# Moving the mixers' two-tensor operations from Pool to DVE in a two-layer network of token mixers

## The chip, the cores and the metric

The kernel runs on one core of a Trainium2 chip. The metric is the device time of one execution in microseconds. Five engines with queues of their own work side by side: TensorE (PE in the profile, with its weight loads as PEld), VectorE (DVE), ScalarE (ACT), GpSimd (POOL, here Pool) and SyncE (SP), which issues nearly all DMAs. Each engine runs its instructions in the order of its queue; an instruction that waits for a semaphore holds up what stands behind it.

## What is computed

The reference is a network of two layers on 256 context and 256 latent tokens of width 1024, in float32. Each layer is: a gated FFN (width 2816) with residual and layer norm; a token mixer; a second FFN. In the last layer only the latent tokens go on.

```
u @ w_in -> columns for three mixers, and three gates
a: gated delta rule, 4 heads, chunks of 128, forward and backward:
   conv + silu of q, k, v; solve (I + A) X = [b v, b exp(g) k];  S = c S + k_w^T u;  o = q S + P u
b: retention with rotary q, k and fixed decays, 4 heads, both directions; head norm; silu gate
c: state-space mixer, 16 heads in 2 groups, both directions:
   o = (scores * decay) (x * step) + decayed state + d * x;  silu gate; group norm
merged = g0 * (ya @ w_a) + g1 * (yb @ w_b) + g2 * (yc @ w_c);   out = merged @ w_out
```

The term `d * x` of mixer c is the skip term.

## The kernel before

Tokens lie along the free axis: 512 columns while both streams are needed, 256 in the second layer where only latent tokens are. Weights come as 1313 blocks of 128x512, in the order of use, through `raw_block` (L104). `wtile` (L113) splits a block: ACT casts it to a high half `whi` (L121), and DVE or Pool subtracts to give the low half `wlo` (L123). Every product is three matmuls (`mm3`, L138): high x high, high x low, low x high. There are four buffers each of `raw`, `whi` and `wlo`; the three steps are emitted with raised priority, so that the planner of the language, which orders each engine's queue from the program's order, priorities and free buffers, sets them ahead of their use.

Who makes `wlo` is decided in L122: of each four blocks, Pool takes the first `pool_lo`. This number is 0 in the FFNs. In the mixers it is set stage by stage from the tuple `plo` (L1435): values of 1 to 4 in the six stages of either layer.

`mix_main` (L1431) orders a mixer. The delta rule (`gdn`, L782) runs first, two heads at a time in layer 0 and four in layer 1; its chain of small operations is filled up with projections of the other mixers: `take(us)` (L502) draws so many microseconds of TensorE work from a generator `fill` (the z gates of mixer a, retention, then the projections of mixer c) and emits it at that place of the program. How much is drawn where stands in `gdn_fill` (L1447). The stages of `gdn`: projections with `conv_silu` (L520; four taps on DVE, L534) and transposes; row vectors written to DRAM (`rows_out`, L767) and read back broadcast over the partitions (`rows_in`, L777) as `Rg` and `Rb`; the matrices M and PT per chunk (L899 to L931), with the product of M with `Rb` on Pool (L925) and that of Q on Pool (L936); 32x32 blocks of M sent through DRAM, loaded as B (L951) and inverted in 31 steps of two DVE operations each (L953 to L959); a merge of the blocks to 128x128 (L993); a scan over four chunks (L1054), whose weighted tiles `bv` and `kw` come from Pool (`weighted`, L967), one chunk ahead in layer 0 and with a single buffer in layer 1.

Then `ssd` (L1218), mixer c, runs interleaved with `merge` (L1374), the gates and the three output products. Per group of heads it loads x as one tile `xt` of 1 MB (L1226), makes weighted values V (L1239) and states (L1253, Pool, and L1254), and per chunk and direction a matrix E of 128 x 8 x 128: decay times score mask (L1289), for the forward direction times step (L1291), then plus DI, the identity times `d` (L1292, on Pool). In `merge` a gated product is added to the sum of the mixers before it on Pool (L1423).

Of the kernel before, what the change touches and what calls it, by code (L numbers as in the profile page):

```python
# [8 lines left out]
F32 = mybir.dt.float32  # L9
# [6 lines left out]
P = 128  # L16
# [30 lines left out]
class Net:  # L47
# [84 lines left out]
    ahead = True  # L132
# [466 lines left out]
    def retention(self):  # L599
# [13 lines left out]
        def table(h):  # L613
# [10 lines left out]
            nc.gpsimd.tensor_tensor(out=tab[:, 1], in0=te2, in1=tab[:, 1], op=ADD)  # L624
# [157 lines left out]
    def gdn(self, H, gp, pool0, gtok):  # L782
# [6 lines left out]
        nu, no = 2 * nh, len(och)  # L789
# [93 lines left out]
        self.take(wt[1])  # L883
# [4 lines left out]
        with ExitStack() as st:  # L888
            pp = st.enter_context(tc.tile_pool(name=f"gprep{tag}", bufs=1, side="right", reuse_waits="tile"))
            for p in range(0, nh, 2):  # L890
                Rg = pp.tile([P, 2, 2, T], F32, tag="Rg", name="Rg")
                Rb = pp.tile([P, 2, 2, T], F32, tag="Rb", name="Rb")
                for d in range(2):
                    self.rows_in(Rg[:, d], self.dR[d * 20 + h0 + p:d * 20 + h0 + p + 2, :])
                    self.rows_in(Rb[:, d], dB[d * nh + p:d * nh + p + 2, :])
                nG = pp.tile([P, 4, 2], F32, tag="nG", name="nG", bufs=2)
                nc.vector.tensor_scalar(out=nG, in0=self.G[:, :, 1, h0 + p:h0 + p + 2], scalar1=-1.0, scalar2=None, op0=MUL)
                pair = lambda t, c: t[:, c].rearrange("p (d h) n -> p d h n", d=2)[:, :, p:p + 2]
                for c in range(4):  # L899
# [25 lines left out]
                    nc.gpsimd.tensor_tensor(out=pair(M, c), in0=pair(M, c), in1=Rb[:, :, :, cs], op=MUL)  # L925
# [6 lines left out]
                for d in range(2):  # L932
                    for i in range(2):
                        q_ = Q[:, d, p + i]
                        nc.scalar.activation(out=q_, in_=Rg[:, d, i, self.oc], func=AF.Exp)
                        nc.gpsimd.tensor_tensor(out=q_, in0=q_, in1=qf[:, p + i], op=MUL)  # L936
# [8 lines left out]
        with ExitStack() as st:  # L945
# [6 lines left out]
            nc.sync.dma_start(out=X, in_=self.io["eye32"].rearrange("(o r) c -> o r c", o=1).broadcast_to([n, 32, 32]))  # L952
            for s in range(31):  # L953
# [5 lines left out]
                self.take(wt[3] / 31)  # L959
# [7 lines left out]
        def weighted(s):  # L967
# [4 lines left out]
            for d in range(2):  # L972
                c, us = ch[d], slice(d * nh, d * nh + nh)
                nc.gpsimd.tensor_tensor(out=bv[:, us], in0=vtok[:, c], in1=bcol(d)[:, c].unsqueeze(2).to_broadcast([P, nh, P]), op=MUL)
                if s < 3:
                    nc.gpsimd.tensor_tensor(out=kw[:, us], in0=ktok[:, c], in1=(w0, w1)[d][:, c].unsqueeze(2).to_broadcast([P, nh, P]), op=MUL)
# [241 lines left out]
    def ssd(self):  # L1218
        nc, l, tc = self.nc, self.l, self.tc
        och, oc = self.och, self.oc  # L1220
        with ExitStack() as st:
            pool = st.enter_context(tc.tile_pool(name=f"ssd{l}", bufs=1, side="right", reuse_waits="tile"))
            for g in range(2):
                hs = slice(4 + 8 * g, 12 + 8 * g)
                xt = pool.tile([P, 4, 512], F32, tag="xt", name="xt")
                nc.sync.dma_start(out=xt, in_=self.dx[:, :, g * 512:(g + 1) * 512].rearrange("c p n -> p c n"))  # L1226
# [4 lines left out]
                def weighted(n):  # L1231
                    for d in range(2):
# [6 lines left out]
                        nc.vector.tensor_tensor(out=v, in0=xt[:, c].rearrange("p (h e) -> p h e", h=8),  # L1239
                                                in1=wv.unsqueeze(2).to_broadcast([P, 8, 64]), op=MUL)  # L1240

                def state(n):
                    for d in sorted(V):
# [7 lines left out]
                        else:  # L1251
                            prev = S[d, c].rearrange("p (h e) -> p h e", h=8)
                            nc.gpsimd.tensor_tensor(out=Sn, in0=prev, in1=self.ct[:, c, d, hs].unsqueeze(2).to_broadcast([P, 8, 64]), op=MUL)  # L1253
# [8 lines left out]
                def prep(c, d):  # L1262
# [27 lines left out]
                    if d == 0:  # L1290
                        nc.vector.tensor_tensor(out=e, in0=e, in1=step.unsqueeze(2).to_broadcast([P, 8, P]), op=MUL)  # L1291
# [519 lines left out]
```

## Time and profile before

| | |
|---|---|
| runs | 2748.7, 2752.3, 2749.12 us; median 2749.12 |
| profiled execution | 2749.3 us, span 2747.5 us |
| TensorE busy | 2594.9 us (94% of the span), granted clock 0.98 on the mean |
| DVE busy | 2068.4 us (75%) |
| ACT busy | 1224.9 us (45%) |
| Pool busy | 719.8 us (26%), of which wlo 291.2 |
| HBM read | 401.93 MB, 158 GB/s with what is written |

The span has two mixers, about 450 to 1112 us and 1990 to 2508 us; before, between and after them lie FFNs. Busy time is the union of an engine's instructions. A wait is idle time of an engine, put down to what ended it. Consecutive DVE instructions overlap a little in the records, so the time from one start to the next is shorter than a duration.

### The profile page before, as it was taken

The page shows a single profiled execution, that of the slowest core. Times are in us where ns is not written, and L with a number is a line of the kernel's source. Part 1 is how long each engine was busy: PE and PEld are TensorE (multiplying, and loading weights), DVE is VectorE, ACT ScalarE, POOL GpSimd, SP SyncE. Part 2 cuts the span into 40 slices and gives each one's busy share as a digit, 9 for nine tenths or more (in the row PEclk, how much of TensorE's full clock was granted, in tenths as well). Part 3 has the DMA queues.
Part 4 walks back from the last instruction along what each step waited for, and adds up shares of the span by engine and source line. Part 5 has one row for each costly group of instructions (what it writes and reads, how often), then busy time and mean ns, then how long its engine had stood idle before and what let it go on. Part 6 is the DMA issues. An engine that isn't in the chain of part 4 may idle for free. (4 is left out here: it accounts for less than half of the span.)

```text
span 2747.5 us, 45507 instructions
## 1 busy us (share of the span) xinstructions
PE 2594.9 (94%) x16136; PEld 2214.7 (81%) x16136; DVE 2068.4 (75%) x4078; ACT 1224.9 (45%) x2420; POOL 719.8 (26%) x615
## 2 busy tenths in 40 slices
PE   8999999999999999999999999999988888888998
PEld 6888887777777778898888988888877778778997
DVE  5888868778878684578888778845788876776766
ACT  3333256443455653363332543323655353654553
POOL 2000054432443253340001320002443433463100
PEclk9999999999999999999999999999999999999999
DMA  8666645422525555365665566643635333756665
GB/s 279 184 185 184 183 139 160 132 63 87 171 78 157 165 169 158 111 196 184 194 186 168 158 205 194 185 117 105 180 101 169 106 97 101 197 183 179 202 184 152
DMA packets 292808, 436.06 MB, mean 159 GB/s; under 512 B 42628, under 2 KB 109700, under 8 KB 292452
## 3 DMA queue, kind: packets, MB, share of 16 engines
q1 hardware_dynamic: 292580, 433.16, 53.6%
q8 instruction: 126, 2.06, 0.3%
q14 instruction: 102, 0.84, 0.1%
HBM read 401.93 MB, written 31.13 MB: 158 GB/s over the span
## 5 line engine op out<-in xcount | busy, mean ns | idle before, releaser
L121 ACT CAST whi<-raw 128x512 fp32r<-128x512 f32 x1003 | 614.9, 618 | 825.1 <-PE pd L142 189.4
L123 DVE TENSOR_TENSOR wlo<-raw,whi 128x512 fp32r<-128x512 f32 x803 | 586.8, 733 | 256.9 <-ACT whi L121 249.8
L141 PE MATMUL p<-uh,whi 128*128 128x512 f32 (+1 forms) x1216 | 445.3, 366 | 1.5 <-ACT whi L121 1.5
L143 PE MATMUL p<-uh,wlo 128*128 128x512 f32 (+1 forms) x1216 | 440.2, 362 | 0.2 <-DVE wlo L123 0.2
L142 PE MATMUL p<-ul,whi 128*128 128x512 f32 (+1 forms) x1216 | 440.2, 362 | 0.0
L123 POOL TENSOR_TENSOR wlo<-raw,whi 128x512 fp32r<-128x512 f32 x200 | 291.2, 1460 | 505.0 <-ACT whi L121 463.9
L190 DVE SCALAR_TENSOR_TENSOR acc<-raw,cT,acc 128x512 f32<-128x512 f32 x448 | 320.4, 753 | 81.3 <-DMA raw<-wst 79.3
L141 PEld LDWEIGHTS p<-uh,whi 128*128 128x128 f32 x1216 | 229.1, 188 | 42.9 <-ACT whi L121 5.0
L307 POOL TENSOR_TENSOR y<-y,piv 128x256 f32<-128x256 f32 x30 | 30.9, 1059 | 884.2 <-ACT piv L305 884.2
L143 PEld LDWEIGHTS p<-uh,wlo 128*128 128x128 f32 x1216 | 229.0, 188 | 37.3 <-DVE wlo L123 0.4
L142 PEld LDWEIGHTS p<-ul,whi 128*128 128x128 f32 x1216 | 229.2, 188 | 34.2
L141 PE MATMUL pd<-ach,whi 128*128 128x512 f32 (+1 forms) x660 | 232.0, 352 | 1.5 <-ACT whi L121 1.5
L143 PE MATMUL pd<-ach,wlo 128*128 128x512 f32 (+1 forms) x660 | 229.4, 348 | 0.5 <-DVE wlo L123 0.5
L142 PE MATMUL pd<-acl,whi 128*128 128x512 f32 (+1 forms) x660 | 229.2, 347 | 0.0
L534 DVE SCALAR_TENSOR_TENSOR cacc<-craw,pcol,cacc 128x508 f32<-128x508 f32 (+2 forms) x192 | 170.7, 894 | 15.7 <-ACT cacc L529 14.1
L141 PEld LDWEIGHTS pd<-ach,whi 128*128 128x128 f32 x660 | 125.0, 189 | 19.0 <-ACT whi L121 2.9
L143 PEld LDWEIGHTS pd<-ach,wlo 128*128 128x128 f32 x660 | 125.0, 189 | 16.7 <-DVE wlo L123 0.9
L142 PEld LDWEIGHTS pd<-acl,whi 128*128 128x128 f32 x660 | 125.0, 189 | 15.2
L141 PE MATMUL gate<-uh,whi 128*128 128x512 f32 (+1 forms) x384 | 132.8, 346 | 0.0
L143 PE MATMUL gate<-uh,wlo 128*128 128x512 f32 (+1 forms) x384 | 130.2, 339 | 1.1 <-POOL wlo L123 1.1
L142 PE MATMUL gate<-ul,whi 128*128 128x512 f32 (+1 forms) x384 | 130.3, 339 | 0.0
L411 ACT CAST ach<-pr 128x512 fp32r<-128x512 f32 (+1 forms) x88 | 50.0, 568 | 141.5 <-DVE pr L410 141.5
(476 smaller groups left out, 6015.3 us busy)
## 6 DMA issues: line engine op xcount, KB each, us to landing
raw<-wst SPq DMA_DIRECT2D x1313, 256.0 KB, 2.8
R<-dR SPq DMA_DIRECT2D x24, 512.0 KB, 5.7
dah<-y SPq DMA_DIRECT2D x9, 1024.0 KB, 5.6
y<-dah SPq DMA_DIRECT2D x28, 256.0 KB, 4.8
Rg<-dR SPq DMA_DIRECT2D x8, 512.0 KB, 4.6
Rb<-dB SPq DMA_DIRECT2D x8, 512.0 KB, 4.9
dx<-xo SPq DMA_DIRECT2D x16, 256.0 KB, 3.1
xt<-dx SPq DMA_DIRECT2D x4, 1024.0 KB, 9.0
```

The source lines that it names most:

```text
L121: nc.scalar.copy(out=hi, in_=r)
L123: e.tensor_tensor(out=lo, in0=r, in1=hi.bitcast(F32), op=SUB)
L141: nc.tensor.matmul(out, wh, xh, start=start, stop=False)
L142: nc.tensor.matmul(out, wh, xl, start=False, stop=False)
L143: nc.tensor.matmul(out, wl, xh, start=False, stop=stop)
L190: eng.scalar_tensor_tensor(out=acc, in0=r, scalar=c, in1=acc, op0=MUL, op1=ADD)
L307: (nc.gpsimd if m >= self.ln_dve[0] else nc.vector).tensor_tensor(out=y[:, m, c], in0=y[:, m, c], in1=piv, op=SUB)
L411: nc.scalar.copy(out=F["ach"][:, m], in_=pr[:, :n])
L534: nc.vector.scalar_tensor_tensor(out=a[:, :, lo:hi], in0=r[:, :, lo + d:hi + d], scalar=w[:, tap:tap + 1], in1=a[:, :, lo:hi], op0=MUL, op ...
```

## The change

All two-tensor operations that the mixers had on Pool go to DVE: `plo` becomes zero everywhere, so DVE makes each `wlo`; the products of M (L925) and Q (L936), the tables of retention (L624), the decayed states (L1253) and the additions of `merge` (L1423) change engine. The weighted tiles of the scan stay on Pool, as one-tensor operations with a scalar per partition, one per head. The skip term is added by the operation that multiplies by step. Three pieces are moved or split: the fill of `gdn_fill[1]` comes behind the first issue of `Rg` and `Rb`; a new entry `gdn_fill[8]` of 8 us (layer 0) or 4 us (layer 1) is taken out of the fill of the 31 steps and put ahead of them; and `xt` is four tiles with four loads.

```diff
-            nc.gpsimd.tensor_tensor(out=tab[:, 1], in0=te2, in1=tab[:, 1], op=ADD)
+            nc.vector.tensor_tensor(out=tab[:, 1], in0=te2, in1=tab[:, 1], op=ADD)
...
         self.rows_out(pool0, 40, 40 + nu, dB)
-        self.take(wt[1])
...
                     self.rows_in(Rb[:, d], dB[d * nh + p:d * nh + p + 2, :])
+                if p == 0:
+                    self.take(wt[1])
...
-                    nc.gpsimd.tensor_tensor(out=pair(M, c), in0=pair(M, c), in1=Rb[:, :, :, cs], op=MUL)
+                    nc.vector.tensor_tensor(out=pair(M, c), in0=pair(M, c), in1=Rb[:, :, :, cs], op=MUL)
...
-                        nc.gpsimd.tensor_tensor(out=q_, in0=q_, in1=qf[:, p + i], op=MUL)
+                        nc.vector.tensor_tensor(out=q_, in0=q_, in1=qf[:, p + i], op=MUL)
...
+            ahead = wt[8]
+            self.take(ahead)
             for s in range(31):
...
-                self.take(wt[3] / 31)
+                self.take((wt[3] - ahead) / 31)
...
-                c, us = ch[d], slice(d * nh, d * nh + nh)
-                nc.gpsimd.tensor_tensor(out=bv[:, us], in0=vtok[:, c], in1=bcol(d)[:, c].unsqueeze(2).to_broadcast([P, nh, P]), op=MUL)
-                if s < 3:
-                    nc.gpsimd.tensor_tensor(out=kw[:, us], in0=ktok[:, c], in1=(w0, w1)[d][:, c].unsqueeze(2).to_broadcast([P, nh, P]), op=MUL)
+                c = ch[d]
+                for i in range(nh):
+                    nc.gpsimd.tensor_scalar(out=bv[:, d * nh + i], in0=vtok[:, c, i], scalar1=bcol(d)[:, c, i:i + 1], scalar2=None, op0=MUL)
+                    if s < 3:
+                        nc.gpsimd.tensor_scalar(out=kw[:, d * nh + i], in0=ktok[:, c, i], scalar1=(w0, w1)[d][:, c, i:i + 1], scalar2=None, op0=MUL)
...
-                xt = pool.tile([P, 4, 512], F32, tag="xt", name="xt")
-                nc.sync.dma_start(out=xt, in_=self.dx[:, :, g * 512:(g + 1) * 512].rearrange("c p n -> p c n"))
+                xt = [pool.tile([P, 512], F32, tag="xt", name="xt", bufs=4) for _ in range(4)]
+                for c in range(4):
+                    nc.sync.dma_start(out=xt[c], in_=self.dx[c, :, g * 512:(g + 1) * 512])
...
-                            nc.gpsimd.tensor_tensor(out=Sn, in0=prev, in1=self.ct[:, c, d, hs].unsqueeze(2).to_broadcast([P, 8, 64]), op=MUL)
+                            nc.vector.tensor_tensor(out=Sn, in0=prev, in1=self.ct[:, c, d, hs].unsqueeze(2).to_broadcast([P, 8, 64]), op=MUL)
...
-                        nc.vector.tensor_tensor(out=e, in0=e, in1=step.unsqueeze(2).to_broadcast([P, 8, P]), op=MUL)
-                        nc.gpsimd.tensor_tensor(out=e, in0=e, in1=DI, op=ADD)
+                        for h in range(8):
+                            nc.vector.scalar_tensor_tensor(out=e[:, h], in0=e[:, h], scalar=step[:, h:h + 1], in1=DI[:, h], op0=MUL, op1=ADD)
...
-                    nc.gpsimd.tensor_tensor(out=a, in0=a, in1=pa[:, :no], op=ADD)
+                    nc.vector.tensor_tensor(out=a, in0=a, in1=pa[:, :no], op=ADD)
...
-        plo = self.plo = ((3, 4, 2, 2, 3, 2), (4, 1, 3, 4, 2, 2))[l]
+        plo = self.plo = ((0,) * 6, (0,) * 6)[l]
...
-            self.gdn_fill = ((2, 4, 5, 18, 1, 1, 3, 4), (2, 4, 5, 20, 0.5, 0.35, 3, 4))[self.outs[0]]
+            self.gdn_fill = ((2, 4, 5, 18, 1, 1, 3, 4, 8), (2, 4, 5, 20, 0.5, 0.35, 3, 4, 4))[self.outs[0]]
```

## Rows read from the trace of the kernel before

**Rows 1.** Stretches (two mixers, an FFN): length, each engine's busy us, PE clock, DMA.
```profile
450.00:1112.00 662.00, 625.02 (x3730) 510.14 (x3730) 494.38 (x1036) 319.89 (x646) 254.56 (x200) 0.98 0.44 129
1990.00:2508.00 518.00, 450.67 (x3512) 400.83 (x3511) 396.44 (x802) 270.88 (x575) 227.06 (x171) 0.96 0.49 141
1250.00:1500.00 250.00, 250.00 (x1243) 201.90 (x1243) 214.71 (x380) 75.37 (x134) 0.00 (x0) 1.00 0.64 187
```

**Rows 2.** Waits of PE, 1940 to 2530 us: total us, times, longest.
```profile
PE rof L687 <- DVE on L681: 7.5, 4, 3.1
...
PE br L143 <- POOL wlo L123: 2.6, 3, 1.2
...
PE gate L143 <- POOL wlo L123: 1.1, 3, 0.6
```

**Rows 3.** Twelve slices of 20 us in which DVE is fullest: their sum.
```profile
sum 240.00, PE 209.47 PEld 170.25 DVE 228.83 ACT 118.77 POOL 121.78; mean PE 17.46 PEld 14.19 DVE 19.07 ACT 9.90 POOL 10.15
```

**Rows 4.** DVE by line and shape: second mixer (two rows), FFN stretch (last row).
```profile
L123 DVE TENSOR_TENSOR wlo<-raw,whi 128x512 fp32r<-128x512 f32 x82 | 67.2, 821 | 35.3 <-ACT whi L121 32.5 <-PE gO L1082 1.2 <-PE br L142 1.1
L534 DVE SCALAR_TENSOR_TENSOR cacc<-craw,pcol,cacc 128x508 f32<-128x508 f32 x36 | 36.0, 999 | 6.7 <-ACT cacc L529 6.4
...
L123 DVE TENSOR_TENSOR wlo<-raw,whi 128x512 fp32r<-128x512 f32 x90 | 61.8, 687 | 4.3 <-ACT whi L121 3.9
```

**Rows 5.** Tiles cacc and E, DVE: shortest, median, longest ns; whole span.
```profile
L534 DVE SCALAR_TENSOR_TENSOR cacc<-craw,pcol,cacc x192: 466/745/1816, 450.6 to 2253.3; 128x508 f32<-128x508 f32 x84, 128x510 f32<-128x510 f32 x84, 128x254 f32<-128x254 f32 x12, 128x255 f32<-128x255 f32 x12
...
L907 DVE SCALAR_TENSOR_TENSOR E<-Rg,G,masks x56: 314/417/1434, 491.3 to 2137.0; 128x128 f32<-128x128 f32 x56
...
L1291 DVE TENSOR_TENSOR E<-E,sp x12: 1210/1224/2318, 872.4 to 2442.7; 128x1024 f32<-128x1024 f32 x12
```

**Rows 6.** Timeline, DVE (four rows) and POOL (three): start us, us, instruction.
```profile
507.47 5.52 DVE L907 SCALAR_TENSOR_TENSOR E<-Rg,G,masks 128x128 f32<-128x128 f32 x5
...
2287.33 2.16 DVE L1069 SCALAR_TENSOR_TENSOR bv<-kS,col,bv 128x128 f32<-128x128 f32 x8 [1.22 <-PE kS L1066]
...
2410.45 0.69 DVE L123 TENSOR_TENSOR wlo<-raw,whi 128x512 fp32r<-128x512 f32 x1 [0.18 <-ACT whi L121]
2411.06 0.68 DVE L1342 TENSOR_TENSOR yscl<-O,ysch 128x512 fp32r<-128x512 f32 x1
...
507.36 1.34 POOL L936 TENSOR_TENSOR Q<-Q,qf 128x512 f32<-128x512 f32 x1
508.67 1.33 POOL L925 TENSOR_TENSOR M<-M,Rb 128x512 f32<-128x512 f32 x1
509.96 2.89 POOL L123 TENSOR_TENSOR wlo<-raw,whi 128x512 fp32r<-128x512 f32 x2
```

**Rows 7.** POOL by line and shape, whole span: busy us, mean ns, idle before.
```profile
L123 POOL TENSOR_TENSOR wlo<-raw,whi 128x512 fp32r<-128x512 f32 x200 | 291.2, 1460 | 505.0 <-ACT whi L121 463.9 <-PE sz L143 11.8 <-ACT mW L1006 9.1
...
L1292 POOL TENSOR_TENSOR E<-E,DI 128x1024 f32<-128x1024 f32 x12 | 29.6, 2464 | 34.9 <-DVE E L1291 34.9
L1423 POOL TENSOR_TENSOR gth<-gth,pa 128x512 f32<-128x512 f32 x16 | 24.4, 1528 | 17.8 <-DVE gth L1419 17.8
```

**Rows 8.** The chain that ended last, second mixer (1990 to 2508 us), by line.
```profile
by line: issue 3.5%; DMA R<-dR 2.6%; POOL wlo L123 1.7%; PE sO L1313 1.3%; PE gate L143 1.2%; PE gate L141 1.2%; PE gate L142 1.2%; POOL gth L1423 1.2%; ACT whi L121 0.9%; DMA yt<-dy 0.8%; PE sS L1246 0.7%; ACT E L1280 0.6%; PE br L142 0.5%
```

**Rows 9.** Waits of DVE, whole span: total us, times, longest.
```profile
DVE tm L956 <- DMA B<-d: 9.4, 3, 5.6
...
DVE E L907 <- DMA Rg<-dR: 3.8, 2, 3.3
...
DVE V L1239 <- DMA xt<-dx: 2.8, 2, 2.5
```

**Rows 10.** POOL: two one-input operations (shortest, median, longest ns), timeline of bv.
```profile
L1029 POOL COPY M<-XX x12: 397/457/1109, 585.9 to 2280.3; 128x256 f32<-128x256 f32 x8, 128x512 f32<-128x512 f32 x4
...
L368 POOL TENSOR_SCALAR y<-y,agb x72: 552/994/2032, 395.0 to 2556.5; 128x256 f32<-128x256 f32 x72
...
2284.52 2.49 POOL L974 TENSOR_TENSOR bv<-gvtok,beta 128x512 f32<-128x512 f32 x2 [3.65 <-PE gU L1074]
```

More of the change, by code (lines that the diff above doesn't have):

```diff
@@ L1238, in weighted @@
                         v = V[d] = pool.tile([P, 8, 64], F32, tag="V", name="V", bufs=2)
-                        nc.vector.tensor_tensor(out=v, in0=xt[:, c].rearrange("p (h e) -> p h e", h=8),
+                        nc.vector.tensor_tensor(out=v, in0=xt[c].rearrange("p (h e) -> p h e", h=8),
                                                 in1=wv.unsqueeze(2).to_broadcast([P, 8, 64]), op=MUL)
@@ L1290, in prep @@
                     if d == 0:
-                        nc.vector.tensor_tensor(out=e, in0=e, in1=step.unsqueeze(2).to_broadcast([P, 8, P]), op=MUL)
-                        nc.gpsimd.tensor_tensor(out=e, in0=e, in1=DI, op=ADD)
+                        for h in range(8):
+                            nc.vector.scalar_tensor_tensor(out=e[:, h], in0=e[:, h], scalar=step[:, h:h + 1], in1=DI[:, h], op0=MUL, op1=ADD)
                     else:
                         xb = units[c][4] = pool.tile([P, 8, 64], F32, tag="V", name="xb", bufs=2)
-                        nc.vector.tensor_tensor(out=xb, in0=xt[:, c].rearrange("p (h e) -> p h e", h=8),
+                        nc.vector.tensor_tensor(out=xb, in0=xt[c].rearrange("p (h e) -> p h e", h=8),
                                                 in1=step.unsqueeze(2).to_broadcast([P, 8, 64]), op=MUL)
@@ L1309, in out @@
                                 if kind == "x":
-                                    lh, rh = xb[:, h] if d else xt[:, c, h * 64:(h + 1) * 64], E[d][:, h]
+                                    lh, rh = xb[:, h] if d else xt[c][:, h * 64:(h + 1) * 64], E[d][:, h]
                                 else:
```

## The prediction

> **What bounds the kernel now.** I read the engines' busy times by stretch first. In an FFN stretch (1250 to 1500 us) TensorE is busy all of the time beside a VectorE (DVE) at 86% and an idle GpSimd (Pool). In the two mixer stretches, 1180 us together, TensorE is idle 37.0 + 67.3 = 104 us, and only there is Pool at work, 254.6 and 227.1 us [rows 1]. All that this change can win lies in those 104 us, and in the dips of the clock beside them (0.98 and 0.96 granted against 1.00). Next, whom TensorE waits for there: DVE results, at the end of chains of small operations, in pieces of 1 to 6 us; for a low half of a weight block (wlo) made by Pool only 3.7 us in six waits of the second mixer [rows 2]. So the low halves come in time; late are the mixers' own chains on DVE.
>
> Then slices of 20 us. In twelve of the 59 slices of the mixers DVE has next to no gap: 228.8 of 240 us. In these TensorE loses 30.5 us, 29% of its mixer idle in 20% of the time [rows 3]. Third, why DVE is full: by operation, with the same tile shapes kept apart. A wlo takes 821 ns in the second mixer and 687 in the FFN stretch without Pool; a convolution tap 999 where the median is 745; an E of the decay 314 at its shortest, and up to 1434 [rows 4, 5]. The timeline shows how: from 507.47 five E's need 5.52 us, where eight such operations in a row take 2.16, a step of (2.16 - 0.34) / 7 = 0.26 us; Pool runs two multiplications and two wlo's just then [rows 6]. DVE and Pool take turns. Such lost time (an operation's duration less the shortest tenth of its form, where a Pool instruction lies over it) comes to 177 us over the two mixers, op by op in the timelines; 170 of it under the kinds of Pool operation that this change removes. From the grouped rows alone it is at least 82 x (0.821 - 0.687) + 36 x (0.999 - 0.745) = 20 us for two groups [rows 4, 5].
>
> **Part 1: two-tensor work from Pool to DVE.** Removed from Pool: 200 wlo, 12 skip additions, 32 merge additions, 16 decayed states, 16 M and 16 Q products and 8 tables three of these seven kinds stand in [rows 7]. On DVE an operation costs the step to the next start, not its duration: 2411.06 - 2410.45 = 0.61 us for 512 columns [rows 6]. So 200 wlo cost 122 us, 56 others of 512 columns 34, 24 of 256 columns (0.33 each: half of the columns' share) 8, 8 tables 4. The skip term becomes eight scalar_tensor_tensor of 128 columns, 8 x 0.26 = 2.08, in place of one step product of 1.22 less the overlap of 0.08 that a wlo of 0.69 has with its successor [rows 5, 6]: 12 x 0.94 = 11. Together +179 us on DVE against 170 that it gets back: no net load, and if nothing came back, +179.
>
> What counts is where. The other 47 slices have DVE gaps, which take up what is moved there; in the last 60 to 70 us of either mixer hardly any time is lost now and some 22 us arrive, beside a TensorE that is nearly full. In the twelve full slices I count 60 us lost and 41 arriving (some 450 operations; [rows 6] are the pattern: 4.2 us lost under four Pool operations that will cost 4 x 0.61 = 2.4). That frees 19 us of DVE where TensorE loses 30.5. A freed DVE lets TensorE on only until the next thing is late (the same slices have ACT and transposes in the chain), so I take half: **-10 us**; bounds -19 and, with nothing given back, +41 less the 11 us of gaps, +30.
>
> A page of the Trainium skill, "SBUF — State Buffer", section "Who interferes with whom", says that a DVE instruction with two SBUF inputs contends with any Pool instruction that reads SBUF. It speaks against a part of this change: the one-input operations left on Pool read SBUF too, and there will be 112 of them where 42 stood. The trace has 1 us or less under Pool's copies, which are few; by the page some of the 7 us now lost under those 42 would stay or double, so the term would be -7 in place of -10.
>
> **Part 2: Pool legs in the chains.** A merge addition has to run on Pool between two DVE operations (1.53 us, now 0.61), a skip addition takes 2.46 behind a product of 1.22 (now 2.08 for both) [rows 5, 7]. In the chain that ended last, over the second mixer, Pool's wlo and gth stand with 1.7% and 1.2% of 518 us [rows 8], 15 us; at half of the duration that is **-8 us**. Bounds 0 (the next wait takes over) and -16 (the first mixer, which the chain does not show this way, gains as much).
>
> **Part 3: work set in front of waits.** No TensorE instruction goes; the order does. In the 31-step solve, DVE stands for the block load B: 9.4 us in three waits [rows 9], and the fill's DVE work stands behind it. Eight (second mixer: four) of the 18 (20) us of fill now go in front; their weight loads, casts and wlo's run during the load. The price is that the solve has less fill left for TensorE, 10 us beside some 16 us of DVE steps; but all of it was DVE's time anyway. The Rg/Rb loads go in front of 4 us of fill on SP's queue: four loads of 512 KB are issued before the fill's two or three weight loads, and what waits on SP behind the Rb load (until dB is written) is those weight loads, with four raw buffers ahead. DVE waited 3.8 us for Rg [rows 9]. Sum of these waits 13.2; I take **-6**, bounds -13 and +6 (the fill that the solve then lacks). The four xt loads in place of one: DVE waited 2.8 us for xt [rows 9], **-2**, bounds -3 and +3 (four issues on SP).
>
> **Part 4: what Pool keeps.** The weighted tiles of the scan become 112 per-head operations of 128 columns. The trace has none. Nearest: a copy of 256 columns 397 ns at its shortest, a two-scalar one 552 [rows 10]; so between half of the latter, 0.28, and all of it, 0.55; I take 0.42, near the copy. In the second mixer, with one buffer, this lies on the path: now two bv from 2284.52 to 2287.0, and DVE uses them at 2287.33 [rows 6, 10]. Eight at 0.42 take 3.4, not 2.5: 0.9 later, two such steps, **+2**; bounds 0 and +7 (if each kw stands before the next head's bv). While Pool is late DVE stands in that step, with wlo's queued behind it. In the first mixer there are two buffers, and it hides.
>
> **Sum.** -10 - 8 - 6 - 2 + 2 = -24. The profiled execution took 2749.3 us (span 2747.5), 0.2 from the median of 2749.12: 2725.3, so 2725. Ends of all terms: -51 and +46.
>
> **Rivals.**
> - *A, slower: DVE becomes the engine that decides in the mixers.* If the long durations are not Pool's doing, or the time comes back where nobody waits, DVE goes from 890.8 to 1070 of 1180 us, and the full slices grow by the +30 of part 1: 2779. Low halves then queue behind DVE's own waits, which Pool's never did. For it: full slices exist; the wlo's come first in the order and push the chains. Against it: 687 ns without Pool. It decides once TensorE's waits for DVE in the mixers pass some 90 us. "Perfetto Trace Analysis" of the Trainium skill, "Optimizing Scalar/DVE Operations", says that offloading from a saturated DVE may make sense, and adds that it might not help between these two; the lost time of the rows bears out the addition.
> - *B, slower by a little: the solve runs out of fill and the per-head operations sit in the scan.* +6 and +7 with parts 1 and 2 at nothing and xt at -2: 2760.
> - *C, no change.* DVE's load is even (179 against 170), and what it gains in one slice the moved wlo's take in the next: parts 1 and 2 cancel with each other's bounds, 2748.
> - *D, a larger gain.* The full slices lose their 30.5 us of idle wholly, the legs give 16, the waits 13: 2749 - 59 = 2690. For it: a chain of ten operations, each 0.3 us shorter, shortens by more than the mean load says. Against: TensorE's many other waits.
>
> **How the numbers follow.** Forecast 0.50, D 0.15, C 0.14, A 0.13, B 0.08. 0.2% is 5.5 us, about what a measurement of this kernel can tell. Forecast and D are faster: 0.65; C 0.14; A and B 0.21. The range reaches to where half of D and half of B are in and A is out: 2695 to 2760. The forecast's own range, which goes by halves of the terms, is 2710 to 2743.
>
> **What would show it.** Right: wlo near 690 ns everywhere in the mixers, taps near 745, E near 340; DVE's busy time in the mixers within 30 us of 891 although it has some 370 more instructions; TensorE's mixer idle down from 104 to about 80; the waits for B, Rg and xt gone. Wrong: DVE busy over 950 there; TensorE waits for DVE wlo that rows 2 do not have; TensorE idle in the solve or the scan of the second mixer where it was not; wlo still at 800 beside Pool's small operations.

## The result and the profile after

The changed kernel takes 2673.63 us (median of 4 runs, 2670.86 to 2685.57); the kernel before, run beside it, 2750.71. The medians differ by 77 us. The ratio of the runs is 0.9735, 95% interval 0.9716 to 0.9754, which is 73 us. The forecast was 24 us less, and its range began at 2695. The direction was right; the forecast size was a third of what came.

The two mixers and an FFN stretch by windows (length, busy us of each engine, granted clock of TensorE, DMA), the mixers cut at the same work as in [rows 1]:

```profile
450.00:1085.00 635.00, 622.96 (x3749) 506.75 (x3749) 490.63 (x1235) 323.63 (x650) 52.94 (x74) 0.99 0.46 135
1963.00:2438.00 475.00, 440.94 (x3517) 396.30 (x3516) 392.57 (x977) 274.34 (x580) 52.44 (x70) 0.97 0.53 155
1220.00:1470.00 250.00, 250.00 (x1243) 201.99 (x1242) 214.09 (x378) 76.73 (x135) 0.00 (x0) 1.00 0.62 189
```

The mixers are 27 and 43 us shorter, 70 of the 77; the FFN stretch is as it was. TensorE's idle time in them falls from 104 us to (635.00 - 622.96) + (475.00 - 440.94) = 46; the other 12 us of the 70 lie in its busy time (1063.9 against 1075.7), at a clock of 0.99 and 0.97 against 0.98 and 0.96. DVE is busy 883 us against 891, with 374 more instructions, and Pool 105 against 482. So DVE took on Pool's work and is no busier: it had lost as much time beside Pool as that work takes.

Whom TensorE waited for shows what was late. Its waits that DVE results ended, summed over the mixers, fall from 87 us to 34. The two longest of before over the whole span stand at transposes of what the convolution chains give; 0.2 us is left of each:

```profile
PE gtr L807 <- DVE vf L537: 13.3, 5, 3.6
PE str L1180 <- DVE sxf L537: 10.7, 6, 4.6
```
```profile
PE gtr L807 <- DVE vf L537: 0.2, 1, 0.2
PE str L1185 <- DVE sxf L537: 0.2, 1, 0.2
```

DVE's operations by line and shape in the second mixer (count, busy us, mean ns, idle before), then two tiles over the whole span (count, shortest, median and longest ns), to be held against [rows 4, 5]:

```profile
L123 DVE TENSOR_TENSOR wlo<-raw,whi 128x512 fp32r<-128x512 f32 x183 | 126.6, 695 | 33.9 <-ACT whi L121 28.9 <-PE sz L143 2.4 <-DMA raw<-wst 0.7
L534 DVE SCALAR_TENSOR_TENSOR cacc<-craw,pcol,cacc 128x508 f32<-128x508 f32 x36 | 26.8, 750 | 0.5 <-ACT cacc L529 0.4
```
```profile
L534 DVE SCALAR_TENSOR_TENSOR cacc<-craw,pcol,cacc x192: 474/742/859, 451.5 to 2197.2; 128x508 f32<-128x508 f32 x84, 128x510 f32<-128x510 f32 x84, 128x254 f32<-128x254 f32 x12, 128x255 f32<-128x255 f32 x12
...
L908 DVE SCALAR_TENSOR_TENSOR E<-Rg,G,masks x56: 341/346/352, 490.3 to 2093.1; 128x128 f32<-128x128 f32 x56
```

The longest tap is 859 ns where it was 1816, the longest E 352 where it was 1434. The lost time, measured as the prediction does (over the mixers, here and below from the first product of mixer a to the first output product), falls from 188 us to 9. Counted to the last ns, such figures below are 0 to 6 us higher; the farthest is d2, 17 in place of 11. A part of the 9 lies under a two-tensor product that stays on Pool, that of the identity with `d` (DI, L1265 of the changed kernel): some 2.8 us.

The twelve 20-us slices of the mixers in which DVE is fullest now, as a sum ([rows 3] before):

```profile
sum 240.00, PE 238.87 PEld 200.16 DVE 237.06 ACT 135.73 POOL 8.98; mean PE 19.91 PEld 16.68 DVE 19.76 ACT 11.31 POOL 0.75
```

This is the row to remember. DVE is fuller than in the twelve slices of before (237 of 240 against 229), and TensorE idles 1.1 us there where it idled 30.5. Two of the slices in [rows 3] were not among the fullest, 560 to 580 us (14.05 us of DVE) and 700 to 720; with 540 to 560 and 740 to 760 in their place the row of before is

```profile
sum 240.00, PE 208.57 PEld 168.97 DVE 233.56 ACT 113.02 POOL 104.18; mean PE 17.38 PEld 14.08 DVE 19.46 ACT 9.42 POOL 8.68
```

and says the same: 31.4 us of idle beside a DVE of 234. So a full DVE by itself does not make TensorE wait.

What TensorE and DVE wait for now (us in all, times, longest; TensorE in the second mixer, DVE over the whole span), for [rows 2, 9]:

```profile
PE sO L1320 <- DVE R L1294: 5.1, 1, 5.1
PE rof L687 <- DVE on L681: 5.0, 2, 4.5
PE str L1185 <- DVE BC L537: 4.6, 1, 4.6
```
```profile
DVE bv L1074 <- POOL bv L979: 3.1, 5, 2.2
DVE V L1246 <- DMA xt<-dx: 3.0, 3, 1.7
DVE E L908 <- DMA Rg<-dR: 2.6, 3, 2.1
DVE M L926 <- DMA Rb<-dB: 2.6, 3, 1.4
```

DVE's wait for the load of B is down from 9.4 us to 1.4. Those for Rg and xt are not gone, Rb is new, since the product of M is now DVE's, and DVE now waits for Pool's bv.

### The profile page after: what moved, and what is told of

Its sections match the earlier page's. It is cut to its first block, busy times and chain, and to the rows that moved or that the text cites. A ratio compares the mean times of both kernels' runs of the same rounds, so it can differ in the third digit from the quotient of the medians.

```text
span 2669.1 us, 45639 instructions
## 1 busy us (share of the span) xinstructions
PE 2577.8 (97%) x16136; PEld 2201.2 (82%) x16136; DVE 2058.9 (77%) x4450; ACT 1228.7 (46%) x2420; POOL 333.5 (12%) x385
## 5 line engine op out<-in xcount | busy, mean ns | idle before, releaser
L123 DVE TENSOR_TENSOR wlo<-raw,whi 128x512 fp32r<-128x512 f32 x1003 | 708.1, 709 | 306.5 <-ACT whi L121 295.3
L534 DVE SCALAR_TENSOR_TENSOR cacc<-craw,pcol,cacc 128x508 f32<-128x508 f32 (+2 forms) x192 | 135.4, 714 | 1.8 <-ACT cacc L529 1.4
L141 PE MATMUL pab<-uh,whi 128*128 128x256 f32 (+1 forms) x288 | 87.8, 312 | 7.9 <-ACT whi L121 4.5
```

Source lines behind the costliest of these rows:

```text
L123: e.tensor_tensor(out=lo, in0=r, in1=hi.bitcast(F32), op=SUB)
L141: nc.tensor.matmul(out, wh, xh, start=start, stop=False)
L534: nc.vector.scalar_tensor_tensor(out=a[:, :, lo:hi], in0=r[:, :, lo + d:hi + d], scalar=w[:, tap:tap + 1], in1=a[:, :, lo:hi], op0=MUL, op ...
```

## The experiments

Theory H/S: Pool's reads hold DVE's operations up; time lost so is dear, since it makes the chains' results late, and the moved wlo's are cheap, since they are made ahead and fill gaps. S at first held that the place matters too: dear in the mixers' chains, cheap in the FFNs. Rival P: time on DVE counts the same, whatever it is, as the prediction's exchange of lost time and load has it. Further rivals: the order (part 3), Pool's legs in the chains (part 2), and weight blocks held up by Pool (theory B of d4, not the prediction's rival B). The first four expectations call them L (lost time), G (the legs) and O (the order). "Lost" is lost time in the mixers; "own work" is DVE's busy time there less it, from the sum over the two mixers in each kernel's windows. Differences between kernels are those of the ratios, times 2749 us; by the ratios' intervals each is uncertain by 5 to 9 us.

| kernel | median us | ratio to before, 95% | lost | own work |
|---|---|---|---|---|
| before | 2750 | 1 | 188 | 736 |
| changed | 2673.63 | 0.9735 [0.9716, 0.9754] | 9 | 908 |
| e1 wlo alone | 2687.07 | 0.9773 [0.9750, 0.9797] | 67 | 851 |
| e2 other operations alone | 2735.36 | 0.9948 [0.9930, 0.9966] | 133 | 791 |
| e3 order alone | 2746.36 | 0.9990 [0.9977, 1.0002] | 184 | 738 |
| e4 all but the order | 2670.19 | 0.9705 [0.9681, 0.9728] | 8 | 907 |
| f1 before, Pool's wlo written only | 2654.37 | 0.9661 [0.9642, 0.9680] | 69 | 739 |
| d1 changed, Pool reads blocks | 2806.18 | 1.0212 [1.0193, 1.0231] | 155 | 900 |
| d2 changed, Pool writes | 2671.94 | 0.9731 [0.9704, 0.9758] | 11 | 907 |
| d3 changed, Pool copies | 2716.32 | 0.9880 [0.9860, 0.9901] | 73 | 901 |
| d4 changed, Pool reads its own tile | 2748.09 | 1.0013 [0.9999, 1.0027] | 106 | 901 |
| f2 changed, no moved wlo on DVE | 2640.66 | 0.9622 [0.9595, 0.9650] | 12 | 796 |
| v3 changed, more DVE work at wlo, half of v1 | 2706.09 | 0.9858 [0.9830, 0.9885] | 10 | 969 |
| v1 changed, more DVE work at wlo | 2752.52 | 1.0006 [0.9989, 1.0023] | 7 | 1033 |
| v2 changed, more DVE work in the taps | 2768.73 | 1.0067 [1.0045, 1.0089] | 10 | 1045 |

**The parts by themselves.** e1 is the kernel before with the wlo's alone on DVE; e2 moves all other operations and leaves the wlo's on Pool; e3 changes only the order (fill in front of the load of B and of the solve, xt in four loads); e4 is the change without e3's part.

```diff
-        plo = self.plo = ((3, 4, 2, 2, 3, 2), (4, 1, 3, 4, 2, 2))[l]
+        plo = self.plo = ((0,) * 6, (0,) * 6)[l]        # e1: this line alone
```
```diff
-                    nc.gpsimd.tensor_tensor(out=pair(M, c), in0=pair(M, c), in1=Rb[:, :, :, cs], op=MUL)
+                    nc.vector.tensor_tensor(out=pair(M, c), in0=pair(M, c), in1=Rb[:, :, :, cs], op=MUL)
...                                                      # e2: this and the other operations, not plo
```
```diff
+            ahead = wt[8]
+            self.take(ahead)                            # e3: the takes and the four xt; e4: the reverse
```

> The kernel before with one edit: DVE makes all wlo, the other operations stay on Pool, no order changed. Theory L (what the change wins is DVE time that was lost in turns with Pool; the 200 wlo lie behind 119 of the 170 us lost): 2750 - 0.7 x 77 = about 2695, and DVE busy in the mixers stays near 890 us. Theory G (the gain is in the Pool legs of the chains, where the wlo hardly stand): 2735 to 2750. Theory O (the gain is in the order): 2750.

> The kernel before with the other engine moves: M, Q, tables, states, merge additions to DVE, skip term in the step products, weighted tiles as one-tensor operations; 200 wlo stay on Pool, no order changed. L: 51 of 170 us lost, 2750 - 0.3 x 77 = about 2727. G: the legs of 88 operations go, 2690 to 2710. O: 2750.

> The kernel before with the order alone: fill behind the Rg/Rb issue, 8 or 4 us of fill ahead of the 31 steps, four xt loads; all engines as before. L and G: the 6 + 2 us of the prediction, 2735 to 2750. O: 2700 or less.

> The changed kernel with the order of before (one xt load, no fill ahead, fill in front of the Rg/Rb issue). L and G: 2674 + 8 = about 2682. O: 2720 or more.

The wlo's alone give 62 us of the 73 that the ratios show, the other operations 14; both together (e4) 81. The order alone gives 2.7 us, within its interval of nothing, and taking it out of the changed kernel does no harm. So the order falls as a cause, and the wlo move carries the result. The legs that the change takes off Pool are off it in e2 and e4 alike, and the wlo move is still worth 67 us between these two; so those legs, standing behind long wlo's, are no cause of it. (For the legs that stay, as bv and kw, see f1.) The wlo move exchanges 121 us of lost time (188 to 67) for 115 us of own work. One for one that is nothing; it gave 62.

**Lost time without load, and load without lost time.** In f1, Pool writes its 200 wlo's in place of computing them: a copy of one column and two memsets, so TensorE multiplies other values. DVE's work is that of before.

```diff
-                e = nc.gpsimd if n % 4 < self.pool_lo else nc.vector
-                e.tensor_tensor(out=lo, in0=r, in1=hi.bitcast(F32), op=SUB)
+                if n % 4 < self.pool_lo:
+                    nc.gpsimd.tensor_copy(out=lo[:, 0:1], in_=hi[:, 0:1].bitcast(F32))
+                    for _ in range(2):
+                        nc.gpsimd.memset(lo.bitcast(F32), 0.0)
+                else:
+                    nc.vector.tensor_tensor(out=lo, in0=r, in1=hi.bitcast(F32), op=SUB)
```

> The kernel before; Pool still makes its 200 wlo, as late in the queue as before, but by writing them (a one-column copy of whi, then two memsets of 512 columns) instead of reading raw and whi: their values are left out. Theory H (Pool's reads hold DVE up, and what DVE loses lies where TensorE waits for it): the 119 us lost under wlo go although nothing moves to DVE, 2690 or less. Theory N (the gain of wlo on DVE is an order that the planner sets better, or wlo that come earlier and free buffers earlier): 2735 to 2750.

The mixers of f1 (sum of both), then of the kernel before and the changed kernel, cut the same way:

```profile
sum 1142.00, PE 1105.67 PEld 941.95 DVE 808.15 ACT 625.93 POOL 479.46; mean PE 552.83 PEld 470.98 DVE 404.07 ACT 312.97 POOL 239.73
```
```profile
sum 1235.00, PE 1128.81 PEld 956.98 DVE 924.56 ACT 624.66 POOL 501.46; mean PE 564.41 PEld 478.49 DVE 462.28 ACT 312.33 POOL 250.73
```
```profile
sum 1165.00, PE 1115.94 PEld 947.41 DVE 917.05 ACT 629.03 POOL 121.34; mean PE 557.97 PEld 473.70 DVE 458.53 ACT 314.52 POOL 60.67
```

Pool is as busy in f1 as before (479 against 501 us), but it reads less, and DVE spends 116 us less on the same instructions. The mixers shorten by 93 us, the whole by 93: 0.78 us for each us not lost. All legs are on Pool here as before, behind nearly as much Pool work, so the legs do not explain it. Nor do blocks that come free earlier, though Pool no longer reads `raw` in f1: ScalarE's waits for loaded blocks are as long in f1 (first row) as before:

```profile
ACT whi L121 <- DMA raw<-wst: 96.1, 62, 5.2
...
ACT whi L121 <- DMA raw<-wst: 102.1, 67, 5.2
```

In f1 1089 of the 16136 matmuls stand at another place than before; d4 below gives a price without that. From f1 to e1 the lost time stays (69 and 67) and 112 us of wlo work come to DVE: 31 us, 0.28 for each (0.20 to 0.35 by the intervals).

f2 does the same on the changed kernel (one memset), where little lost time is left:

> The changed kernel without DVE's load of the 200 moved blocks: Pool writes their wlo by a copy of one column and a memset (the subtraction is left out, so TensorE multiplies other values); Pool's reads stay as few as in the changed kernel. DVE loses some 125 us of work in the mixers. Theory S (work at the place of wlo is cheap as long as DVE has gaps): 0.27 x 125 = 34 us less, about 2640. Theory P (it counts like any DVE time, 0.6 as v1 or 0.8 as lost time): 75 to 100 us less, 2575 to 2600.

```profile
sum 1126.50, PE 1102.12 PEld 940.71 DVE 807.67 ACT 627.24 POOL 282.57; mean PE 551.06 PEld 470.36 DVE 403.83 ACT 313.62 POOL 141.28
```

112 us of own work less than the changed kernel, and 31 us less time: again 0.28. f1 and f2 multiply zeros in these blocks; whether that changes TensorE's time by itself was not tried. In f2, 14 of the 31 us lie in TensorE's busy time (1102 against 1116), so the 0.28 is less sure than its two equal values make it look.

**Pool's idle work in the changed kernel: what holds DVE up.** Behind the 200 blocks Pool does work that nobody uses: two subtractions of 256 columns of the block (d1), four memsets (d2), three copies (d3), two subtractions on a tile of its own (d4).

```diff
+                if n % 4 < self.pool_lo:                # d1; plo as before
+                    for i in range(2):
+                        c = slice(i * 256, i * 256 + 256)
+                        nc.gpsimd.tensor_tensor(out=self.dum, in0=r[:, c], in1=hi[:, c].bitcast(F32), op=SUB)
...
+                    nc.gpsimd.tensor_copy(out=self.dum[:, 0:1], in_=hi[:, 0:1].bitcast(F32))
+                    for _ in range(4):                  # d2
+                        nc.gpsimd.memset(self.dum, 0.0)
...
+                    for _ in range(3):                  # d3
+                        nc.gpsimd.tensor_copy(out=self.dum, in_=hi[:, 0:256].bitcast(F32))
...
+                    for _ in range(2):                  # d4, behind d2's copy of one column
+                        nc.gpsimd.tensor_tensor(out=self.dum, in0=self.dum, in1=self.dum, op=SUB)
```

> The changed kernel (DVE makes all wlo); Pool in addition does, for the 200 blocks that were its own, two subtractions of 256 columns of raw and whi into a scratch tile that nobody reads: idle work. H: DVE loses 100 us and more again, and time goes from 2674 back to 2735 or above. N: 2674 to 2685 (raw is held a little longer).

> As the run before, but Pool's idle work reads one column of whi and then only writes: four memsets of 256 columns, as long as the subtractions. H with reads as what holds DVE: DVE loses next to nothing, 2670 to 2680. If Pool's writes hold DVE too: 2720 or more. N: 2674.

> As the run before, with three copies of 256 columns of whi per block as Pool's idle work: one input. H: one-input operations read as well, so DVE loses a share like that of the subtractions, 2710 to 2735. If only two-input operations of Pool hold DVE: 2670 to 2685. N: 2674 to 2685.

> The changed kernel as in d1, but Pool's idle subtractions (2 x 256 columns for each of the 200 blocks) read and write a tile of Pool's own; only a copy of one column ties them to the block. Nothing of the block is held by them. Theory H (Pool's reads hold DVE's operations up, whatever they read): as d1, 110 to 150 us more than the changed kernel, 2785 to 2825. Theory B (d1's time came from blocks held longer, so that the next one is loaded late): 0 to 20 us more, 2674 to 2694.

Pool's idle operations in d2, d3, d4 and d1 (count, busy us, mean ns), and under each the taps on DVE (shortest, median, longest ns):

```profile
L127 POOL MEMSET dum<- 128x256 f32 x800 | 250.3, 313 | 46.1
```
```profile
L538 DVE SCALAR_TENSOR_TENSOR cacc<-craw,pcol,cacc x192: 470/740/857, 449.8 to 2195.9; 128x508 f32<-128x508 f32 x84, 128x510 f32<-128x510 f32 x84, 128x254 f32<-128x254 f32 x12, 128x255 f32<-128x255 f32 x12
```
```profile
L126 POOL COPY dum<-whi 128x256 f32<-128x256 f32 x600 | 431.8, 720 | 585.3 <-ACT whi L122 558.1
```
```profile
L537 DVE SCALAR_TENSOR_TENSOR cacc<-craw,pcol,cacc x192: 468/737/941, 448.8 to 2243.5; 128x508 f32<-128x508 f32 x84, 128x510 f32<-128x510 f32 x84, 128x254 f32<-128x254 f32 x12, 128x255 f32<-128x255 f32 x12
```
```profile
L128 POOL TENSOR_TENSOR dum<-dum 128x256 f32<-128x256 f32 x400 | 342.8, 857 | 31.6
```
```profile
L539 DVE SCALAR_TENSOR_TENSOR cacc<-craw,pcol,cacc x192: 467/739/1182, 448.9 to 2259.8; 128x508 f32<-128x508 f32 x84, 128x510 f32<-128x510 f32 x84, 128x254 f32<-128x254 f32 x12, 128x255 f32<-128x255 f32 x12
```
```profile
L127 POOL TENSOR_TENSOR dum<-raw,whi 128x256 f32<-128x256 f32 x400 | 437.4, 1093 | 659.9 <-issue 330.8 <-ACT whi L122 295.8 <-POOL dum L127 13.1
```
```profile
L538 DVE SCALAR_TENSOR_TENSOR cacc<-craw,pcol,cacc x192: 467/737/1284, 449.3 to 2303.9; 128x508 f32<-128x508 f32 x84, 128x510 f32<-128x510 f32 x84, 128x254 f32<-128x254 f32 x12, 128x255 f32<-128x255 f32 x12
```

Memsets beside DVE cost nothing that can be told (a difference of 1 us, with 390 us more of Pool's time in the mixers); copies cost 40 us, two-input operations 76 and 131. In d2, d3 and d4 the instructions of TensorE, DVE and ScalarE stand in the changed kernel's order, one by one, so no new order is in these prices. d4 against d2 is the cleanest pair: the same order, the same copy of one column, and no more of the block held; only memsets have become two-input operations, on a tile of Pool's own. So d4's 76 us are DVE's longer operations. Over the mixers d4 has

```profile
sum 1239.30, PE 1138.86 PEld 963.30 DVE 1007.10 ACT 629.35 POOL 579.61; mean PE 569.43 PEld 481.65 DVE 503.55 ACT 314.68 POOL 289.81
```

that is, 100 us of TensorE idle, where the changed kernel has 49 by the row under f1, d2 44, d3 82 and d1 145; the rest of each difference lies in TensorE's busy time. TensorE's waits for DVE are 82 us in d4 and 29 in d2. Where d1 loses more than d4, 146 us more than the changed kernel against 97, it also takes longer on Pool and holds the blocks, and 571 of its 16136 matmuls stand in another order. Time for each us lost: d1 131 / 146 = 0.90, d3 40 / 64 = 0.62, d4 76 / 97 = 0.79, f1 0.78. d4 falls short of the 110 us that theory H named, but it is far from B's 20: its lost time is two thirds of d1's, and so is its cost.

"SBUF — State Buffer" of the Trainium skill, section "Who interferes with whom", says that a DVE instruction with two SBUF inputs contends with a Pool instruction that reads SBUF, and not with one that only writes it. The runs agree: copies with one input lose DVE 64 us, memsets, which read nothing, 2 us. Under the one-input products of bv and kw that the change keeps on Pool, some 2.4 of the 9 us are still lost, as the prediction's sentence on the page had it; no run prices that.

**More work on DVE.** v1 puts idle subtractions on DVE at the place of the moved wlo's, v3 half as many, v2 about as many as v1 behind the first operation of each chain of taps.

```diff
+                    for i in range(2):                  # v1, behind the moved wlo; v3: one
+                        c = slice(i * 256, i * 256 + 256)
+                        nc.vector.tensor_tensor(out=self.dum, in0=r[:, c], in1=hi[:, c].bitcast(F32), op=SUB)
...
+            for _ in range(2):                          # v2, in conv_silu
+                nc.vector.tensor_tensor(out=self.dum, in0=raw[:, 0], in1=acc[:, 0], op=SUB)
```

> The changed kernel with idle work on DVE where the change put work: behind the wlo subtraction of each of the 200 blocks that Pool used to make, DVE makes two more subtractions of 256 columns of the same block into a tile that nobody reads, some 400 times 0.33 us = 132 us in the mixers; Pool is untouched. Theory S (load put at the place of wlo has slack, as e1 minus f1 says: 33 us of time for 122 us of DVE work): 0.27 x 132 = 35 us more than the changed kernel, about 2710. Theory P (the prediction's: DVE load counts like any other DVE time, at the 0.79 that f1 showed for lost time): 105 us more, about 2780. TensorE's idle time in the mixers grows by the same amounts.

> The changed kernel with the same sort of idle DVE work at another place: two subtractions of 256 columns behind the first operation of each of the 192 chains of conv taps, 384 times 0.33 us = 127 us, which the steps of those chains wait for. Theory S (time in the chains comes out at about 0.8, time at wlo at about 0.3): 100 us more than the changed kernel, about 2775, against 2710 for v1. Theory P (any DVE time counts alike): v1 and v2 come out within 10 us of each other.

> v1 with one idle subtraction of 256 columns for each of the 200 blocks in place of two: 66 us more DVE work in the mixers. If the price of such work rises as DVE's gaps fill (0.27 below the changed kernel's load, v1's 0.6 as a mean above it): 18 to 33 us more than the changed kernel, about 2700. If idle work behind wlo has one price of 0.6 throughout: 40 us more, about 2714. If v1 had lost its time to another order alone: anywhere from 0 to 80.

v1 cost 75 us for 124 us of own work, 0.60; S had said 35, P 105. v3 cost 34 for 61, 0.56, and from v3 to v1 it is 0.64; the intervals do not tell 0.56 from 0.64. Against f2's 0.28 below the changed kernel's load, work above it is twice as dear: S's flat 0.27 was wrong, and its reason (gaps that work made ahead can fill) would fit a price that rises as DVE fills, but the order changes too. v2 cost 91 for 137, 0.67, not three times v1's price, as S had it, and by the intervals hardly to be told from it. So above this load the place in the program, chains or wlo, mattered little, if at all. P had the sizes no better: v2 is 17 us above v1, not within 10. TensorE waits in v2 where S said, at the taps:

```profile
PE sx L142 <- ACT cacc L530: 15.9, 9, 5.4
PE str L1188 <- DVE BC L540: 12.2, 4, 4.6
PE str L1188 <- DVE sxf L540: 11.6, 5, 4.9
```

The planner orders TensorE anew for such work (in v1, place by place, 4317 of its 16136 matmuls are others than in the changed kernel), so a part of these prices may be order.

**Pool's work outside the mixers.** c1 is d1's work, and c2 d4's, for every third block outside the mixers (221 of them).

```diff
+                if self.outside and n % 3 == 0:         # c1 as d1, c2 as d4
```

> The changed kernel with Pool made busy outside the mixers: idle two-input subtractions of 2 x 256 columns for every third weight block there, some 185 of them, as many as the 200 in the mixers that cost 132 us in d1. DVE's operations beside them are held up as much each. Theory S (the lost time is dear only where it falls on the mixers' chains; in the FFNs DVE has much time to spare): at most 15 us more, 2674 to 2689. Theory P (each us that Pool holds DVE up costs the same anywhere): 80 to 130 us more, 2755 to 2805.

> The changed kernel as in c1 (Pool busy outside the mixers, every third block), again on a tile of Pool's own. In c1 ScalarE waited 400 us for loaded blocks, against 85 in the changed kernel, so c1's 101 us may come from blocks held by Pool. Theory S (lost time costs little where few chains wait for DVE, c1 was the held blocks): 0 to 20 us more, 2674 to 2694. Theory P (lost time costs the same wherever it falls): 80 to 110 us more, 2755 to 2785, with ScalarE's waits for loaded blocks near 85 us.

c1 took 2774.55 us (1.0088, 1.0066 to 1.0111), c2 2736.32 (0.9966, 0.9953 to 0.9979): 97 and 63 us more than the changed kernel for 129 and 75 us more lost outside the mixers, 0.75 and 0.84. Theory S's part on the place falls: lost time is as dear outside the mixers. Theory B does not explain it, since Pool holds no block in c2, and the order of TensorE, DVE and ScalarE is the changed kernel's in both. P did not have c2 right either: it set 80 to 110 us, with ScalarE's waits for loaded blocks near 85. In c2 ScalarE waits for loaded blocks 285 us, where the changed kernel has 85:

```profile
ACT whi L123 <- DMA raw<-wst: 284.8, 146, 8.4
```
```profile
ACT whi L121 <- DMA raw<-wst: 85.2, 62, 5.4
```

A raw buffer comes free when DVE has read it; with DVE held up, the loads and casts behind it come late. That reading fits the rows, but no run isolates it.

**Two single edits, and a better version.** w1 is e4 with bv and kw as two-tensor products on Pool again, s1 is e4 with the skip term as a product and an addition on DVE, n1 is e4 with the norms' two-input operations on DVE as well.

```diff
-                for i in range(nh):                     # w1
-                    nc.gpsimd.tensor_scalar(out=bv[:, d * nh + i], in0=vtok[:, c, i], scalar1=bcol(d)[:, c, i:i + 1], scalar2=None, op0=MUL)
+                nc.gpsimd.tensor_tensor(out=bv[:, us], in0=vtok[:, c], in1=bcol(d)[:, c].unsqueeze(2).to_broadcast([P, nh, P]), op=MUL)
...
-                        for h in range(8):              # s1
-                            nc.vector.scalar_tensor_tensor(out=e[:, h], in0=e[:, h], scalar=step[:, h:h + 1], in1=DI[:, h], op0=MUL, op1=ADD)
+                        nc.vector.tensor_tensor(out=e, in0=e, in1=step.unsqueeze(2).to_broadcast([P, 8, P]), op=MUL)
+                        nc.vector.tensor_tensor(out=e, in0=e, in1=DI, op=ADD)
...
-            (nc.vector if m < 2 else nc.gpsimd).tensor_tensor(out=ym, in0=ym, in1=rb, op=MUL)
+            nc.vector.tensor_tensor(out=ym, in0=ym, in1=rb, op=MUL)     # n1, and ln_dve, and the last norm
```

> The version of e4 with the weighted tiles (bv, kw) made by Pool's two-tensor products again, 16 of four or eight heads in place of 112 per-head ones. The prediction's part 4 put the per-head form at 2 us (0 to 7) dearer, so 0 to 7 us less than e4's 2670 here if Pool's length is what counts. Theory H (two-input reads hold DVE up; lost time costs 0.77): each two-tensor product is some 8 x 0.7 us of such reads less what the long form saves; at the 97 us lost for 343 us of Pool's two-input time in d4, 50 to 80 us of products lose DVE 14 to 23 us, 11 to 18 us more than e4, 2681 to 2688.

> The version of e4 with the skip term as a product and an addition of the whole 1024-column tile on DVE in place of eight step products of one head each. The work on DVE is of like length (two times 1.2 us against eight times 0.3 us for each of 40 tiles). Both theories expect no change: 2665 to 2675. More than 10 us either way would say that the form of the products, not their load, had a price that no theory here holds.

> The version of e4 (the changed operations in the earlier order) in which DVE makes the norms' two-input products and additions too, so that Pool has no two-input operation left anywhere. In e4 some 42 us of DVE time are still lost beside Pool's norm operations, and some 46 us of load move to DVE. Theory S (a lost us in a chain is worth more than a moved one): 10 to 20 us less than e4's 2670, so 2650 to 2660. Theory P (one for one): no change, 2665 to 2675. A loss would say that the norms' chains are themselves what TensorE waits for and that Pool carried part of them beside DVE.

w1: 2670.83 (0.9718, 0.9694 to 0.9742); s1: 2665.55 (0.9704, 0.9676 to 0.9732). Neither can be told from e4. (s1 changes 12 tiles, not the 40 of the expectation.) In w1 only 5 us more were lost, not 14, so 4 us are what 0.78 gives, and 4 is the difference of the ratios; my expectation had put the products' length too high. n1: 2651.76 us (0.9648, 0.9624 to 0.9671), 16 us under e4, as expected: lost time outside the mixers falls from 52 to 4 us. It is the fastest of the versions that leave nothing out, 24 us under the changed kernel by the ratios.

## Why the prediction was wrong

- **What bounds the kernel** was read rightly: the mixers, the chains on DVE, operations held up by Pool. Its signs came: wlo at 695 ns, taps at 742, E at 346, DVE's busy time 8 us from 891. TensorE's idle time went past its sign, to 46 where 80 stood, and of the waits for B, Rg and xt only that for B went, to 1.4 us. Both sizes of part 1 were right too: 177 us lost (179 went), 179 us of work arriving (908 - 736 = 172).
- **Part 1 is the step that failed.** It set the two against each other one for one ("no net load"), counted only the twelve full slices, 60 us lost and 41 arriving, and took half: -10, bounds -19 to +30. The reason it gave was that elsewhere DVE's gaps take up what changes. For the arriving wlo's that is nearly so: they cost 0.28 each us. For lost time it is not: it costs 0.6 to 0.9 in every place tried, inside the mixers and outside, and TensorE's waits for DVE results rise and fall with it (87 us before, 34 after, 22 in f1, 82 in d4). So the sum of this case is 179 x 0.78 = 140 us gained, 112 x 0.28 = 31 paid for the wlo's, and for the other 60 us of work 32, at the 0.53 that e2 shows ((55 x 0.78 - 14) / 55): 77 us in all, where the ratio gave 73. All three prices come from runs of this kernel, the last from e2 itself, so the sum is no independent test.
- The evidence was in the rows. Twelve slices held a fifth of the mixers' time and 29% of TensorE's idle, 60 of the 177 us; 117 us lost elsewhere were counted at nothing, with 71% of the idle time beside them. Two readings were a little off and change none of this: the twelve slices were not quite the fullest, and in the last 70 us of the second mixer 8.5 us are lost, more than "hardly any".
- **Part 2** (-8) can't be told apart: e2's 14 us hold the legs, 55 us of lost time and 55 us of load. **Part 3** (-6 and -2) is not to be seen: -2.7, interval -6.3 to +0.5, alone, and no gain within the change. The wait for B went, but not by part 3: with the order alone (e3) it stays, and without the order (e4) it is as short as in the changed kernel; the rows stand below. So the engine moves shortened it, by what path is open. The waits for Rg and xt stayed, 2.6 and 3.0 us where 3.8 and 2.8 stood. **Part 4** took 0.42 us for a per-head product. The timeline of the changed kernel below shows eight in 5.08, 0.64 each, and DVE waiting for them; w1 shows that this costs nothing that can be measured.

The wait for B in e3, in e4 and in the changed kernel, then the timeline:

```profile
DVE tm L960 <- DMA B<-d: 9.7, 3, 5.3
...
DVE tm L956 <- DMA B<-d: 1.6, 1, 1.6
...
DVE tm L960 <- DMA B<-d: 1.4, 1, 1.4
```
```profile
2226.83 5.08 POOL L979 TENSOR_SCALAR bv<-gvtok,beta 128x128 f32<-128x128 f32 x8 [3.95 <-PE gU L1079]
...
2229.62 2.09 DVE L1074 SCALAR_TENSOR_TENSOR bv<-kS,col,bv 128x128 f32<-128x128 f32 x7 [2.16 <-POOL bv L979]
```

- **The rivals.** D came nearest to the mechanism: a chain of ten operations shortens by more than the mean load says, and the full slices lost their idle. It had a chance of 0.15 and stopped at 2690, because its largest term too looked at these slices only. A, B and C are out: the kernel is faster, DVE is not busier, and TensorE's longest wait for a wlo of DVE is 0.9 us.

What stays open is why a us lost to Pool (0.6 to 0.9) is so much dearer than one of the moved wlo work (0.28), while work added on top of it, at wlo (0.56 to 0.64) or in the taps (0.67), comes near the lower end of the lost time. Work is known to the planner, which orders around it, and time lost beside Pool is not; that is a guess that no run isolates.

## What to carry to other kernels

When an engine's operations take longer beside another's, count most of that lost time (here 0.6 to 0.9 of it) wherever it falls, since it delays results; count work moved in its place by the gaps that it goes to, and little where it is made ahead and the engine has gaps. Compare TensorE's idle with DVE's *late results*, not with its fullness: a slice can be 99% full and harmless. Before moving work by load, try what the other engine costs merely by running: replacing its operations by memsets of about the same length shows it in one run, as f1 did here.

## What the hardware showed

- Pool's operations hold DVE up by their reads, not by their time: 512 us of Pool's work in the mixers with memsets lose DVE 11 us, 547 with copies 73, 580 with two-input operations on one tile 106, 555 with those on two tiles of the block 155.
- A one-scalar product of 128 columns on Pool takes 0.64 us in a row, more than the 0.55 taken as an upper bound from a two-scalar one of 256 columns at its shortest [rows 10].
